# The last down projection of a two-layer decoder trunk: seven of eight output tiles in two passes over the tokens, with split weights kept between the passes

## The chip, the cores and the metric

The kernel runs on one core of one Trainium2 chip. The metric is the device time of one execution in microseconds (us). A core has a matrix engine (TensorE, "PE" in the profile), a vector engine (VectorE, "DVE"), a scalar engine (ScalarE, "ACT"), a general engine (GpSimd, "POOL") and a queue processor that issues transfers (SyncE, "SP"). Matrix products accumulate in eight PSUM banks of 128 partitions x 512 float32; everything else lies in SBUF.

## The reference

Two layers of a decoder trunk over 512 tokens with 1024 channels. What matters here is the end of each layer, the SwiGLU block with 2816 hidden units, and the norm behind the last layer:

```python
        x = x + mix @ w_out[l]
        h = rms_norm(x, norm_ffn_w[l])
        x = x + (jax.nn.silu(h @ ffn_w_gate[l]) * (h @ ffn_w_up[l])) @ ffn_w_down[l]
    return rms_norm(x, final_norm_w)
```

`rms_norm` divides each token by the root of the mean square of its 1024 channels, so no token of the output is known before all channels of that token are.

## The kernel before

**Layout.** Activations stand with channels on the partitions: `x[0..7]` are eight tiles of 128 channels x 512 tokens. The 22 tiles of hidden units (`KF`) have the tokens along their free side too. Each float32 product is made of three products of rounded halves (`mm3`, L447 to L452: high weights by high activations, high by low, low by high). A weight tile therefore comes by a DMA into a `wraw` buffer (`w_load`, L337 on, five buffers, SP's queue), ACT casts its high half `whi` (L256), and POOL or DVE subtracts for the low half `wlo` (L257). PE then takes 128 columns of `whi` or `wlo` as its loaded weights and streams 256 or 512 tokens past them.

**The feed-forward block** of each layer runs the list `steps`: hidden tiles 0 to 3 by plain products (`hidden_plain`), then the down projection of hidden tiles 0 and 1 (`head`) for all eight outputs, then hidden tiles 4 to 21 and the down projection of hidden tiles 2 to 17 by a scheme that replaces eight block products by seven (`step`, L1585 on: products e, t1, t2, g, h, t3, t4 in PSUM pool `pm`; t4 of one step is put off until `finish()` in the next), and last the down projection of hidden tiles 18 to 21 (`rest`): `down_plain(1)`, L1650 on. Its products accumulate in pool `pd`, which has four PSUM banks. For each output tile it takes the next split weights (`w_next`), makes 4 x 3 matmuls per token range, adds the sum to `x[m]` (L1665), squares the result on ACT (`ssq_add`, L220), adds the squares up in `ssq` on DVE (L222) and scales `x[m]` by the norm's weight on ACT (L1675). Output tile 0 takes its weights in two runs of two hidden tiles; between them `finish()` makes the last t4, and with it hidden tile 21.

**The order of the last layer** comes from `down_order` (L260): output tiles 0 to 5 over all tokens, then tiles 6 and 7 over the first 256 tokens, then tiles 6 and 7 over the last 256 tokens. For the second half the weights of tiles 6 and 7 are loaded and split a second time.

**The end of the kernel.** For one half of the tokens, `rstd_sum` (L226 on) sums the squares over channels by matmuls with one column (L230), scales the sum on DVE (`ms`, L234) and takes the power -1/2 on POOL (`rst`, L212). `leave` (L1637 on) spreads the result over the partitions by matmuls (`rstd_spread`, L241), copies it to SBUF on ACT (`rsb`, L245), multiplies the eight tiles, five on DVE (L1647) and three on POOL (L1645), and issues eight output DMAs, alternately from SP and ACT (L1648). The first half's sum is written behind the matmuls of tile 6's second half, its `leave` behind those of tile 7's second half; the second half's come after all.

**Weights ahead of time.** `items` is the list of all split weights in order, `pieces` that of all DMAs. `w_next` hands out item i, splits the next two, and within a feed-forward block splits up to `AHEAD` = 5 items ahead, but only items of the seven-product scheme (tuples of two). Those are spread over two SBUF pools of four slots, `wsp` and the block's own `ffw` (the list `extra`); plain items use `wsp` alone. An item of the scheme that is a difference of weight blocks (`s1`, `s2`, `s4`) is computed by DVE into a `pd` bank.

**Who sets the order.** The code writes instructions in the order described, and the program is built with a planner that orders each engine's instructions by its own estimates of their durations (`schedule_with_timeline_sim=True`). The order on an engine can thus differ from the order in the text of the kernel.

Of the kernel before, what the change touches and what calls it, by code (L numbers as in the profile page):

```python
# [8 lines left out]
F32R = mybir.dt.float32r  # L9
# [7 lines left out]
P = 128  # L17
T = 512
NB = T // P
D = 1024  # L20
KD = D // P
# [5 lines left out]
DEPTH = 2  # L27
# [3 lines left out]
EU, ET = 0, 0  # L31
N_OUT = 4
R_SUM = [1, 0]
TAIL = 2
CONF_POOL = 7
CHUNK_K = 2
ARENA = 43
# [10 lines left out]
AHEAD = 5  # L48
# [89 lines left out]
def kernel(  # L138
# [15 lines left out]
    V, S, GP, PE = nc.vector, nc.scalar, nc.gpsimd, nc.tensor  # L154
# [5 lines left out]
    wsp = ctx.enter_context(tc.tile_pool(name="wsp", bufs=4))  # L160
# [89 lines left out]
        S.activation(xh[k], x[k], AF.Copy, scale=col(wcol + k))  # L250
        V.scalar_tensor_tensor(xl[k], x[k], col(wcol + k), xh[k].bitcast(F32), op0=MUL, op1=SUB)  # L251

    def split_w(r, n=512, eng=GP):
        hi = wsp.tile([P, 528], F32R, name="whi")
        lo = wsp.tile([P, 528], F32R, name="wlo")
        S.copy(hi[:, :n], r)  # L256
        eng.tensor_tensor(lo[:, :n], r, hi[:, :n].bitcast(F32), op=SUB)  # L257
        return hi, lo

    def down_order(l):  # L260

        full, hv = slice(0, T), [slice(0, T // 2), slice(T // 2, T)]
        n = TAIL if l == DEPTH - 1 else 0
        return [(m, full) for m in range(KD - n)] + [(m, c) for c in hv for m in range(KD - n, KD)] * (n > 0)

    pieces, items = [], []
# [16 lines left out]
    def plain_order(l, end):  # L285
        return down_order(l) if end else [(m, slice(0, T)) for m in range(KD)]
# [5 lines left out]
    for l in range(DEPTH):  # L292
        for nm in ORDER:
            if nm == "gg":
                for g in range(2):
                    plain(wg[l, g], 4 * (G + 2 * H))
            elif nm in T_GROUPS:
                for g in range(2):
                    plain(wt[l, 2 * T_GROUPS.index(nm) + g], 4 * G)
            else:  # L300
                plain(wc[l, C_TILES.index(nm)], KD * P)
        for m, g in OUT_ORDER:
            plain(wo[l, m][:, g * 4 * P:(g + 1) * 4 * P], 4 * P)
        left = None
        for what, *n in steps:
            if what == "plain":
                for n_m, (m, _) in enumerate(plain_order(l, *n)):
                    for r in runs(*n, n_m == 0):
                        plain(wd[l, m][:, r[0] * P:(r[-1] + 1) * P], len(r) * P)
                        if left is not None:  # L310
                            items.append(("d", left))
                            left = None
                continue
            if what == "hidden":
                two = [wf[l, 2 * n[0] + q] for q in range(2)]
                if n[0] < N_PLAIN:
                    for ap in two:
                        plain(ap, KD * P, (V, GP))
                    continue
            else:  # L320
                part, q = n
                k0 = HEAD + part * PART
                two = [wd[l, m][:, k0 * P:(k0 + PART) * P] for m in (2 * q, 2 * q + 1)]
            pj = len(pieces)
            pieces.extend((ap, KD * P) for ap in two)
            for u in ("a", "s1", "d", "s2", "b", "s4", "s3"):
                if u != "d":
                    items.append((u, pj))
                elif left is not None:
                    items.append((u, left))  # L330
            left = pj
    raws, halves, sums = {}, {}, {}
    pos = [0, 0, 0]
# [14 lines left out]
    def slots(pool):  # L348
        return held.setdefault(id(pool), [])
# [37 lines left out]
    def w_split(upto):  # L387
        while pos[1] < min(upto, len(items)):
            i, it = pos[1], items[pos[1]]
            if len(it) == 3:  # L390
                p, n, eng = it
                h = n // 2 if n > 1024 else 512
                if len(slots(wsp)) + (n + h - 1) // h > 4:
                    return
                w_load(p + 1)
                r = raws.pop(p)
                late = i >= len(items) - 2 * TAIL
                halves[i] = []
                for a in range(0, n, h):
                    slots(wsp).append(i)  # L400
                    halves[i].append(split_w(r[:, a:min(a + h, n)], min(h, n - a), V if late and a == 0 else eng[a > 0]))
            else:
                pools = [q for q in (*extra, wsp) if len(slots(q)) < 4]
                if not pools:
                    return
                w_load(it[1] + 2)
                s_item(i, *it, min(pools, key=lambda q: len(slots(q))))
            pos[1] += 1

    def w_next():  # L410
        i = pos[2]
        pos[2] += 1
        for q in held.values():
            q[:] = [n for n in q if n >= i]
        p = piece_of(items[i])
        w_split(i + 1)
        assert i in halves
        w_load(p + 3)
        w_split(i + 2)
        while pos[1] < min(i + 1 + AHEAD, len(items)) and len(items[pos[1]]) == 2 and extra:  # L420
            n = pos[1]
            w_split(n + 1)
            if pos[1] == n:
                break
            w_load(piece_of(items[n]) + 3)
        return halves.pop(i)
# [1014 lines left out]
    for l in range(DEPTH):  # L1441
# [47 lines left out]
        with tc.tile_pool(name=f"ffp{l}", bufs=1, reuse_waits="tile") as ffp, \  # L1489
# [160 lines left out]
            def down_plain(rows):  # L1650
                order = plain_order(l, rows)
                js = (head, rest)[rows]
                for n_m, (m, c) in enumerate(order):
                    ps = pd.tile([P, T], F32, name="pd")[:, c]
                    for r in runs(rows, n_m == 0):
                        hv = w_next()
                        for n, k in enumerate(r):
                            ph, pl = hid[k]
                            mm3(ps, *hv[n // 4], n % 4, ph[:, c], pl[:, c], k == js[0], k == js[-1])
                        finish()  # L1660
                    if rows and l + 1 == DEPTH and n_m == KD:
                        rstd_sum(range(NB // 2), ssq)
                    if rows and l + 1 == DEPTH and n_m == KD + 1:
                        leave(0)
                    V.tensor_tensor(x[m][:, c], x[m][:, c], ps, op=ADD)  # L1665
                    if not rows:
                        continue
                    if l + 1 < DEPTH:
                        split_x(m, o + NV + V_NMIX)
                        ssq_add(m)  # L1670
                        nc.sync.dma_start(xs[m * P:(m + 1) * P, :], x[m])
                    else:
                        end = n_m == len(order) - 1
                        sq = ssq_add(m, end, c)
                        S.activation(x[m][:, c], x[m][:, c], AF.Copy, scale=col(V_FIN + m))  # L1675
                return sq if rows and l + 1 == DEPTH else None
# [99 lines left out]
```

## Time and profile before

| | |
|---|---|
| time, median of 3 runs | 1346.11 us (1344.49 to 1348.75) |
| the profiled execution: its time | 1343.3 us |
| its span, first to last instruction | 1341.5 us |
| mean granted PE clock | 0.978 of full speed |
| PE busy | 1288.5 us, 96% |
| DVE, ACT, POOL busy | 67%, 52%, 60% |
| DMA | 124.53 MB, mean 93 GB/s |

The profile reads one execution on the chip. Busy times of PE add up overlapping instructions, since matmuls are pipelined: from one matmul's start to the next one's is the better measure of its price. In a timeline a row has its start, its duration, engine, line, operation, output and inputs, shapes and count, and in brackets how long the engine stood idle before it and what ended that idle time. A view of windows gives each engine's busy time in a stretch, with the granted PE clock ("PEclk") and the share of the DMA engines.

### The profile page before, as it was taken

Reading aid. Unit: us, or ns where it says so; the run is one execution under the profiler, and the core shown is the slowest. Engines: PE = TensorE matmul, PEld = TensorE weight load, DVE = VectorE, ACT = ScalarE, POOL = GpSimd, SP = SyncE. Lnnn points to the kernel's source line nnn. Section 1 sums busy time; section 2 is a strip of 40 time slices with the busy share of each in tenths; the row PEclk is TensorE's granted clock in tenths of the full one; section 3 lists DMA queues with packets and bytes.
Section 4 is the critical chain, followed back from the end, with each engine's and each line's share of the span. In section 5 each row is a group of like instructions: output and inputs, shape, how many; then the busy total and the mean of one; then the engine's idle time right before and its main releaser. Section 6 shows DMA issues by size and latency. Waiting matters only on the chain.

```text
span 1341.5 us, 23755 instructions
## 1 busy us (share of the span) xinstructions
PE 1288.5 (96%) x8984; PEld 1176.6 (88%) x8984; DVE 895.0 (67%) x1569; ACT 703.9 (52%) x1454; POOL 802.4 (60%) x669
## 2 busy tenths in 40 slices
PE   8899988999999999999999998989999999999996
PEld 6788987978889999999878887888788999999995
DVE  5652769646888857776466357676559787678645
ACT  5453454535556655665446344535445566566554
POOL 5376674844366765676445766748634667566662
PEclk8899988999999999999999998989999999999998
DMA  7224210134143332332433222102422333233332
GB/s 261 68 70 115 66 40 9 33 109 134 38 151 96 110 98 92 108 113 80 154 130 95 74 78 70 29 1 64 146 86 88 101 124 112 85 125 96 106 87 71
DMA packets 60243, 124.53 MB, mean 93 GB/s; under 512 B 17504, under 2 KB 26976, under 8 KB 60128
## 3 DMA queue, kind: packets, MB, share of 16 engines
q1 hardware_dynamic: 58688, 121.83, 29.6%
q8 instruction: 71, 1.16, 0.4%
q10 hardware_dynamic: 1440, 1.18, 0.3%
q14 instruction: 44, 0.36, 0.1%
HBM read 116.17 MB, written 6.82 MB: 92 GB/s over the span
## 4 chain that ended last, share of the span: by engine, by line
PE 82%; DVE 9%; POOL 3%; ACT 3%; issue 2%; DMA 1%; POOLq 0%; SPq 0%; ACTq 0%; DVEq 0%
PE pm L450 12%; PE pm L452 12%; PE pm L451 12%; PE pd L450 10%; PE pd L451 10%; PE pd L452 10%; PE pd L480 3%; PE pd L479 3%; PE pd L478 3%; PE pm L1147 1%; POOL wlo L257 1%; DVE x L1250 1%; PE pm L886 1%; DVE ph L1518 1%; PE pm L1040 1%
## 5 line engine op out<-in xcount | busy, mean ns | idle before, releaser
L257 POOL TENSOR_TENSOR wlo<-wraw,whi 128x512 fp32r<-128x512 f32 (+2 forms) x192 | 255.0, 1335 | 248.3 <-ACT whi L256 246.8
L380 POOL TENSOR_TENSOR wlo<-wraw,whi 128x512 fp32r<-128x512 f32 x208 | 276.3, 1346 | 103.1 <-ACT whi L379 93.2
L450 PE MATMUL pm<-bh,whi 128*128 128x256 f32 x1008 | 283.1, 283 | 6.6 <-ACT pm L1599 3.1
L451 PE MATMUL pm<-bl,whi 128*128 128x256 f32 x1008 | 280.8, 280 | 0.0
L452 PE MATMUL pm<-bh,wlo 128*128 128x256 f32 x1008 | 276.8, 280 | 0.0
L256 ACT CAST whi<-wraw 128x512 fp32r<-128x512 f32 (+2 forms) x212 | 125.2, 598 | 195.7 <-PE pd L451 124.3
L450 PEld LDWEIGHTS pm<-bh,whi 128*128 128x128 f32 x1008 | 189.7, 188 | 11.4 <-ACT pm L1599 4.8
L451 PEld LDWEIGHTS pm<-bl,whi 128*128 128x128 f32 x1008 | 190.1, 189 | 0.5
L452 PEld LDWEIGHTS pm<-bh,wlo 128*128 128x128 f32 x1008 | 187.9, 189 | 0.4 <-DVE wlo L380 0.3
L450 PE MATMUL pd<-xh,whi 128*128 128x512 f32 x416 | 166.5, 402 | 4.2 <-DVE pm L935 2.3
L451 PE MATMUL pd<-xl,whi 128*128 128x512 f32 x416 | 166.3, 401 | 1.3 <-DVE xl L251 1.3
L452 PE MATMUL pd<-xh,wlo 128*128 128x512 f32 x416 | 165.7, 400 | 0.0
L379 ACT CAST whi<-wraw 128x512 fp32r<-128x512 f32 x208 | 126.4, 626 | 48.8 <-PE pm L451 41.9
L380 DVE TENSOR_TENSOR wlo<-pd,whi 128x512 fp32r<-128x512 f32 x156 | 107.0, 687 | 43.3 <-ACT whi L379 41.1
L379 ACT CAST whi<-pd 128x512 fp32r<-128x512 f32 x156 | 92.1, 590 | 78.4 <-PE pm L451 30.0
L374 POOL TENSOR_TENSOR wraw<-wraw 128x512 f32<-128x512 f32 x52 | 69.6, 1339 | 70.7 <-DVE pd L362 52.3
L478 PE MATMUL pd<-whi,xh 128*128 128x256 f32 (+1 forms) x320 | 94.5, 297 | 7.3 <-DVE ar L583 6.2
L450 PEld LDWEIGHTS pd<-xh,whi 128*128 128x128 f32 x416 | 79.5, 191 | 23.2 <-ACT ar L1050 2.4
L451 PEld LDWEIGHTS pd<-xl,whi 128*128 128x128 f32 x416 | 79.5, 191 | 20.1 <-DVE xl L251 2.9
L452 PEld LDWEIGHTS pd<-xh,wlo 128*128 128x128 f32 x416 | 79.6, 191 | 17.6
L479 PE MATMUL pd<-wlo,xh 128*128 128x256 f32 (+1 forms) x320 | 94.5, 296 | 0.0
L480 PE MATMUL pd<-whi,xl 128*128 128x256 f32 (+1 forms) x320 | 93.7, 295 | 0.0
(354 smaller groups left out, 3113.5 us busy)
## 6 DMA issues: line engine op xcount, KB each, us to landing
wraw<-in_wf_dram SPq DMA_DIRECT2D x88, 512.0 KB, 3.7
wraw<-in_wc_dram SPq DMA_DIRECT2D x35, 512.0 KB, 3.6
wraw<-in_wd_dram SPq DMA_DIRECT2D x32, 512.0 KB, 3.6
wraw<-in_wt_dram SPq DMA_DIRECT2D x16, 512.0 KB, 3.5
wraw<-in_wo_dram SPq DMA_DIRECT2D x32, 256.0 KB, 2.6
x<-in_xt_dram SPq DMA_DIRECT2D x16, 256.0 KB, 4.5
wraw<-in_wd_dram SPq DMA_DIRECT2D x16, 256.0 KB, 2.7
wraw<-in_wd_dram SPq DMA_DIRECT2D x20, 128.0 KB, 2.0
```

The costliest lines, as they stand in the source:

```text
L256: S.copy(hi[:, :n], r)
L257: eng.tensor_tensor(lo[:, :n], r, hi[:, :n].bitcast(F32), op=SUB)
L374: GP.tensor_tensor(src, c, a, op=SUB)
L379: S.copy(hi, src)
L380: eng.tensor_tensor(lo, src, hi.bitcast(F32), op=SUB)
L450: PE.matmul(ps, hi[:, w], ah, start=first, stop=False, skip_group_check=shared)
L451: PE.matmul(ps, hi[:, w], al, start=False, stop=False, skip_group_check=shared)
L452: PE.matmul(ps, lo[:, w], ah, start=False, stop=last, skip_group_check=shared)
L478: PE.matmul(o, xh[k][:, tk], hi[:, w], start=(k == 0 and b % per == 0), stop=False)
L479: PE.matmul(o, xh[k][:, tk], lo[:, w], start=False, stop=False)
L480: PE.matmul(o, xl[k][:, tk], hi[:, w], start=False, stop=(k == KD - 1 and b % per == per - 1))
L886: PE.matmul(pq[:, ct * 2 * P:(ct + 1) * 2 * P], kq[ct][rr_, b, 0, :], kq[ct][rr_, b, :, :], start=True, stop=True)
```

## The change

`TAIL` goes. In the last layer the order of the last down projection becomes: output tile 0 over all tokens, tiles 1 to 7 over the first 256 tokens, then tiles 1 to 7 over the last 256. The split weights of tiles 1 to 7 are kept in their slots from the first pass to the second (`kept`, and `w_next(keep)`, which doesn't give the slots of the last `keep` items free), so those of tiles 6 and 7 are no longer loaded and split twice: 9 pieces in place of 11. Plain items of at most 512 columns may now lie in `ffw` too, whichever of the two pools has more room, and are split up to five items ahead in a feed-forward block, as those of the scheme are. This holds in both layers, for the down projections of `head` and of `rest`. Every second one of the last eight items has its low half made by DVE. The first half's sum is written behind the matmuls of the first tile of the second pass (`n_m == KD`), its `leave` behind those of the fourth (`n_m == KD + 3`).

```diff
-TAIL = 2
...
-    def split_w(r, n=512, eng=GP):
-        hi = wsp.tile([P, 528], F32R, name="whi")
-        lo = wsp.tile([P, 528], F32R, name="wlo")
+    def split_w(r, n, pool, eng):
+        hi = pool.tile([P, 528], F32R, name="whi")
+        lo = pool.tile([P, 528], F32R, name="wlo")
...
         full, hv = slice(0, T), [slice(0, T // 2), slice(T // 2, T)]
-        n = TAIL if l == DEPTH - 1 else 0
-        return [(m, full) for m in range(KD - n)] + [(m, c) for c in hv for m in range(KD - n, KD)] * (n > 0)
+        if l < DEPTH - 1:
+            return [(m, full) for m in range(KD)]
+        return [(0, full)] + [(m, c) for c in hv for m in range(1, KD)]
...
-                for n_m, (m, _) in enumerate(plain_order(l, *n)):
+                for n_m, (m, c) in enumerate(plain_order(l, *n)):
+                    if c.start:
+                        continue
...
                 h = n // 2 if n > 1024 else 512
-                if len(slots(wsp)) + (n + h - 1) // h > 4:
+                pool = wsp
+                if n <= 512 and extra:
+                    pool = min((*extra, wsp), key=lambda q: len(slots(q)))
+                if len(slots(pool)) + (n + h - 1) // h > 4:
                     return
...
-                late = i >= len(items) - 2 * TAIL
+                late = i >= len(items) - KD and i % 2
...
-    def w_next():
+    def w_next(keep=0):
+
         i = pos[2]
         pos[2] += 1
         for q in held.values():
-            q[:] = [n for n in q if n >= i]
+            q[:] = [n for n in q if n >= i - keep]
...
-        while pos[1] < min(i + 1 + AHEAD, len(items)) and len(items[pos[1]]) == 2 and extra:
+        while pos[1] < min(i + 1 + AHEAD, len(items)) and extra and (len(items[pos[1]]) == 2 or items[pos[1]][1] <= 512):
...
                 js = (head, rest)[rows]
+                kept = {}
                 for n_m, (m, c) in enumerate(order):
                     ps = pd.tile([P, T], F32, name="pd")[:, c]
                     for r in runs(rows, n_m == 0):
-                        hv = w_next()
+                        if c.start:
+                            hv = kept[m]
+                        else:
+
+                            hv = kept[m] = w_next(len(kept) if c.stop < T else 0)
+                            if n_m == 0:
+                                kept.clear()
                         for n, k in enumerate(r):
                             ph, pl = hid[k]
                             mm3(ps, *hv[n // 4], n % 4, ph[:, c], pl[:, c], k == js[0], k == js[-1])
                         finish()
                     if rows and l + 1 == DEPTH and n_m == KD:
                         rstd_sum(range(NB // 2), ssq)
-                    if rows and l + 1 == DEPTH and n_m == KD + 1:
+                    if rows and l + 1 == DEPTH and n_m == KD + 3:
                         leave(0)
```

More of the change, by code (lines that the diff above doesn't have):

```diff
@@ L396, in w_split @@
                 r = raws.pop(p)
-                late = i >= len(items) - 2 * TAIL
+                late = i >= len(items) - KD and i % 2
                 halves[i] = []
                 for a in range(0, n, h):
-                    slots(wsp).append(i)
-                    halves[i].append(split_w(r[:, a:min(a + h, n)], min(h, n - a), V if late and a == 0 else eng[a > 0]))
+                    slots(pool).append(i)
+                    halves[i].append(split_w(r[:, a:min(a + h, n)], min(h, n - a), pool, V if late and a == 0 else eng[a > 0]))
             else:
```

## The prediction

> **What bounds the kernel now.** I read the page first, then the windows around the end, then each engine's timeline there. The page, busy shares and chain that ended last:
>
> ```profile
> PE 1288.5 (96%) x8984; PEld 1176.6 (88%) x8984; DVE 895.0 (67%) x1569; ACT 703.9 (52%) x1454; POOL 802.4 (60%) x669
> ...
> PE 82%; DVE 9%; POOL 3%; ACT 3%; issue 2%; DMA 1%; POOLq 0%; SPq 0%; ACTq 0%; DVEq 0%
> ```
>
> PE has the chain for 82% of the span. A change that neither takes matmuls away nor fills PE's pauses can gain only where PE stands still. The view of windows shows where that is at the end:
>
> ```profile
> 1308.00:1314.00 6.00, 5.05 (x29) 4.05 (x27) 0.82 (x2) 0.58 (x1) 0.00 (x0) 1.00 0.00 0
> 1314.00:1320.00 6.00, 6.00 (x27) 4.91 (x28) 4.98 (x8) 4.60 (x9) 2.56 (x2) 1.00 0.18 45
> 1320.00:1328.00 8.00, 8.00 (x60) 7.57 (x59) 7.18 (x14) 7.72 (x16) 0.00 (x0) 1.00 0.00 0
> 1328.00:1335.00 7.00, 3.15 (x22) 2.73 (x20) 2.64 (x9) 1.48 (x4) 3.44 (x5) 0.82 0.41 134
> 1335.00:1341.50 6.50, 0.04 (x1) 0.00 (x0) 1.75 (x5) 0.37 (x1) 2.09 (x3) 0.50 0.55 182
> ```
>
> The columns are stretch, length, PE, PEld, DVE, ACT, POOL, clock, DMA. PE is full until 1328 but for 0.95 us around 1313. From 1328 to the end, 13.5 us, no engine is full: that is a chain of small steps. PE's timeline gives its pieces:
>
> ```profile
> 1305.39 0.40 PE L451 MATMUL pd<-ph,whi 128*128 128x512 f32 x1
> ...
> 1310.72 0.39 PE L450 MATMUL pd<-ph,whi 128*128 128x512 f32 x1
> 1310.95 0.28 PE L450 MATMUL pm<-bh,whi 128*128 128x256 f32 x1
> ...
> 1312.22 0.28 PE L452 MATMUL pm<-bh,wlo 128*128 128x256 f32 x1
> 1312.33 0.39 PE L451 MATMUL pd<-ph,whi 128*128 128x512 f32 x1
> 1312.56 0.40 PE L452 MATMUL pd<-ph,wlo 128*128 128x512 f32 x1
> 1313.90 1.19 PE L450 MATMUL pd<-ph,whi 128*128 128x512 f32 x4 [0.95 <-ACT ph L1517]
> ...
> 1316.79 0.39 PE L450 MATMUL pd<-ph,whi 128*128 128x512 f32 x1
> ...
> 1319.76 0.39 PE L452 MATMUL pd<-ph,wlo 128*128 128x512 f32 x1
> ...
> 1325.11 0.28 PE L450 MATMUL pd<-ph,whi 128*128 128x256 f32 x1
> ...
> 1327.85 0.28 PE L452 MATMUL pd<-ph,wlo 128*128 128x256 f32 x1
> 1327.97 0.51 PE L230 MATMUL pm<-cs,ssq 128*128 128x1 f32 x4
> 1329.83 0.71 PE L241 MATMUL pm<-cs,rst 128*128 128x128 f32 x4 [1.35 <-POOL rst L212]
> 1330.37 0.50 PE L230 MATMUL pm<-cs,ssq 128*128 128x1 f32 x4
> 1330.74 0.58 PE L230 MATMUL pm<-cs,sq 128*128 128x1 f32 x4
> 1333.82 1.22 PE L241 MATMUL pm<-cs,rst 128*128 128x128 f32 x4 [2.50 <-POOL rst L212]
> ```
>
> The last large matmul starts at 1327.85. Behind it both halves' statistics run one behind the other: sum (L230) and spread (L241) of the first half, then of the second. The other engines, first DVE, then ACT, then POOL:
>
> ```profile
> 1328.17 0.42 DVE L1665 TENSOR_TENSOR x<-x,pd 128x256 f32<-128x256 f32 x1 [0.64 <-PE pd L452]
> ...
> 1328.84 0.15 DVE L234 TENSOR_SCALAR ms<-pm 128x2 f32<-128x2 f32 x1
> 1330.98 1.75 DVE L1647 TENSOR_TENSOR x<-x,pm 128x256 f32<-128x256 f32 x5 [1.98 <-ACT rsb L245]
> 1332.64 0.15 DVE L234 TENSOR_SCALAR ms<-pm 128x2 f32<-128x2 f32 x1
> 1335.48 1.75 DVE L1647 TENSOR_TENSOR x<-x,pm 128x256 f32<-128x256 f32 x5 [2.69 <-ACT rsb L245]
> ```
>
> ```profile
> 1328.62 0.42 ACT L220 ACTIVATE sq<-x 128x256 f32<-128x256 f32 x1 [0.44 <-DVE x L1665]
> ...
> 1330.57 0.37 ACT L245 COPY rsb<-pm 128x256 f32<-128x256 f32 x1 [0.99 <-PE pm L241]
> ```
>
> ```profile
> 1329.08 0.70 POOL L212 TENSOR_TENSOR rst<-ms,mhalf 128x2 f32<-128x2 f32 x1 [10.42 <-DVE ms L234]
> 1331.02 2.09 POOL L1645 TENSOR_TENSOR x<-x,rsb 128x256 f32<-128x256 f32 x3 [1.25 <-ACT rsb L245]
> 1333.07 0.69 POOL L212 TENSOR_TENSOR rst<-ms,mhalf 128x2 f32<-128x2 f32 x1
> ```
>
> The second half's squares are ready at 1328.62 + 0.42 = 1329.04, but its `ms` waits until 1332.64 behind the first half's five multiplications on DVE, and its `rst` until 1333.07 behind POOL's three. The second half stands in line behind the first on three engines.
>
> **The change part by part.** The profiled execution took 1343.3 us for a span of 1341.5, so 1.8 lie around it; the median is 1346.1, 2.8 more. I make the sum against the profiled one and carry the difference over to the median.
>
> *The end (gain).* The first half is complete after the first pass, 7 tiles before the last matmul, and its `leave` is written four tiles before the end. Its multiplications, copy and DMA issues then lie beside matmuls. The last half's chain stands alone. From the start of the last large matmul: add to `x` at 0.32 (1328.17), square from 0.77 to 1.19 (1328.62), sum of the squares 0.58 with a pick-up of about 0.04, to 1.81; `ms` 0.04 + 0.15, to 2.00; `rst` 0.09 + 0.70, to 2.79; spread 0.05 + 0.71, to 3.55; copy 0.03 + 0.37, to 3.95; first multiplication at 3.99. Before, it is 1335.48 - 1327.85 = 7.63. What follows (multiplications, DMAs, 1341.5 - 1335.48 = 6.02) is the same. **-3.64.**
>
> For the spread I took the first row (0.71 at 1329.83), not the second (1.22 at 1333.82). PE had stood for 1.35 us before the one and 2.50 before the other, and the clock was 0.82 and then 0.50 in the two last windows. In the new chain PE stands for under a microsecond between square and sum and about one before the spread, like the first row. The Trainium skill, "TensorE: Matmul & The Clock Gate", Part 1 on the clock gate, puts the step at a window of about 3.4 us with little activity, free-running, after which PE has half its clock. The trace agrees with a halving (0.50). By that rule a window that falls badly could still halve the spread: my sum would then be 0.5 smaller.
>
> *PE's stream (loss).* Tiles 1 to 5 change from 12 matmuls of 512 tokens to 24 of 256. Between 1316.79 and 1319.76 lie 13 steps of 512, 0.228 each; between 1325.11 and 1327.85 lie 23 of 256, 0.119 each. A pair costs 0.010 more, 5 x 12 = 60 pairs **+0.6**. Sum and spread of the first half, which stood behind the last matmul, now stand in the stream: 1330.74 - 1330.37 = 0.37 and 1330.37 - 1329.83 = 0.54, **+0.9**; the chain that feeds them (about 2.8 us from add to `rst`) is covered by three tiles of 12 x 0.119 = 1.43.
>
> *The pause at 1313 (open).* Hidden tile 21 comes from the t4 product, the 12 matmuls from 1310.95 to 1312.22:
>
> ```profile
> 1305.99 0.43 DVE L1609 TENSOR_TENSOR pm<-pm,u 128x256 f32<-128x256 f32 x1 [2.00 <-ACT u L1608]
> 1312.53 0.70 DVE L1622 TENSOR_TENSOR pm<-pm,sg 128x512 f32<-128x512 f32 x1 [6.11 <-PE pm L452]
> ```
>
> Until its halves are ready at 1313.90, PE fills in the products of hidden tiles 18 to 20, as far as four `pd` banks go: four tiles x 9 = 36 matmuls, 24 of them in one row from 1305.39 to 1310.72 and two behind t4; the other ten lie before that. After the change three of the four banks hold half tiles: 9 x 0.228 + 27 x 0.119 = 5.3 us of filling in place of 8.2, **2.95 less**. The matmuls aren't lost, they come later; the question is only whether PE stands meanwhile. After ten early ones some 3.1 are left. To be covered are the wait before t4 (the filling starts at 1305.39, L1609 ends at 1306.42, 1.0) and that from t4's last matmul to 1313.90, 1.7. So 3.1 would cover 2.7 if the planner split it well: -0.95 (the pause goes). If, as now, nearly all of it is put ahead of t4, the pause becomes about 1.5: +0.5. Below both, if t4 itself could not start before 1310.9, the whole 2.95 would show. I take **+0.5**, the order of the row, and keep -0.95 and +2.95 as ends. Behind it PE needs a fifth bank about 1.8 us after 1313.90 in place of 2.9, while the add that frees the first is no earlier than before:
>
> ```profile
> 1315.59 2.48 DVE L1665 TENSOR_TENSOR x<-x,pd 128x512 f32<-128x512 f32 x4 [1.02 <-PE pd L452]
> ```
>
> One add is 0.62; I give that **+0.2**, between 0 and 0.6.
>
> *Weights.* The first pass takes a weight tile every 1.43 us instead of every 2.8. With eight slots and five items ahead, they can be split in the stretch from 1305 to 1313, where DVE, ACT and POOL are nearly idle (0.82, 0.58 and 0.00 busy of 6 us from 1308). Two pieces fewer are split. ACT and DVE were off the path there, so this is worth 0; if the cover fails, a cast and a subtraction (below 2 us) show once.
>
> *Elsewhere.* The earlier splitting also holds for the `head` down projection in both layers and for `rest` in the first. PE, as the windows show, stands for almost nothing there, while DVE is full:
>
> ```profile
> 1010.00:1020.00 10.00, 10.00 (x44) 8.10 (x44) 10.00 (x19) 5.25 (x11) 3.00 (x2) 1.00 0.08 26
> 1020.00:1030.00 10.00, 10.00 (x45) 8.15 (x44) 10.00 (x20) 5.01 (x12) 3.38 (x5) 1.00 0.18 52
> 1030.00:1040.00 10.00, 9.85 (x49) 8.01 (x48) 9.83 (x20) 5.83 (x14) 7.73 (x8) 1.00 0.70 213
> ```
>
> There is nothing to gain and something to lose: the scheme's differences s1 and s2 are now made about four items earlier, on a full DVE, and hold `pd` banks that the `head` tiles want. I take 0; the ends are -1 and +6 (two layers, two tiles of 6 x 0.228 = 1.4 each, that PE would wait for).
>
> **Sum:** -3.64 + 0.6 + 0.9 + 0.5 + 0.2 = **-1.4 us**, 1341.9 against 1343.3, or **1344.7** against the median of 1346.1.
>
> **The rivals.**
>
> *1. The pause goes.* The planner puts t4 ahead of the filling, and banks don't hold PE up: -1.4 - 0.95 - 0.5 - 0.2 = -3.1, 1343.0. For it: 3.1 us of filling for 2.7 of waits. Against: the order of before, 24 in a row ahead of t4, though L1609 was done at 1306.42.
>
> *2. Half tiles starve PE (the other side).* At 1305 to 1314 the four `pd` banks are filled with half as much work, and t4's start is set by something other than the row of matmuls ahead of it. The 2.95 show in full instead of 0.5: -1.4 + 2.45 = +1.0, 1347.2, slower than before. It decides from a pause 1.9 longer than now. For it: PE did have all 36 fillers in and still stood for 0.95. Against: nothing that t4 reads is seen to end later than 1306.42.
>
> *3. The `head` stage pays.* Banks taken by s1 and s2 hold PE up near 1035 and at the same place of the first layer, and the shifted order reaches into the second layer's mixers. +4 or so on the sum, 1349. Against it, PE could take the scheme's products meanwhile, which don't need `pd`.
>
> *4. It doesn't do what it says:* the planner leaves the first half's `leave` behind the last matmul. Then 7.63 stays and PE's stream costs 0.6 + 0.5 + 0.2: +1.3, 1347.4. Against: those squares are complete some 8 us before the end.
>
> **How the numbers follow.** Forecast 0.55, rival 1 0.20, rival 2 0.14, rival 3 0.08, rival 4 0.03. A measurement of this kernel tells about 0.3%, 4.0 us, from no change (its three runs lie 4.3 apart). Even rival 1 is only 0.23%, so faster by over 0.3% needs rival 1 and luck in the medians or a shift elsewhere: 0.15. Slower by over 0.3% is most of rival 3 and a little of 2 and 4 with the runs' spread: 0.12. Within: 0.73. The range takes rival 1 with a microsecond elsewhere and the medians' scatter at the low end (1340.5), rivals 2 and 3 at the high end (1349).
>
> **What would show it.** Right: L1647 and L1645 for the first half before the last L452; from the last L452 to the second L1647 about 4.0; matmuls of 256 at 0.119 with L230 and L241 among them; fewer `pd` matmuls ahead of t4. The pause before hidden tile 21's products separates forecast (about 1.5), rival 1 (near 0) and rival 2 (near 3.9). PE's busy time from 1000 to 1060 and in the first layer's same stage judges rival 3. The prediction would be wrong by a last chain much over 4 (an engine late with work from the second pass: ACT has there seven squares of 0.42, seven scalings and four DMA issues), or by any shift over 4 us ahead of 1290, which I cost at nothing.

## The result, and the profile after

| | before | after |
|---|---|---|
| time, median of 14 runs each | 1344.87 us (1343.39 to 1348.75) | 1351.91 us (1348.09 to 1358.29) |
| ratio | 1 | 1.0055, 95% interval 1.0043 to 1.0067 |
| profiled execution, its span | 1343.3, 1341.5 us | 1356.9, 1355.1 us |

The change makes the kernel slower by 0.55%, 7.0 us between the medians. The forecast was 1.4 us faster, and its range ended at 1349.0. The profiled execution of after is one of its long ones, 5 us above its median. So the difference of the two profiles, 13.6 us, is more than the change costs; I use the profiles for where and how, and the medians for how much.

The page of after: busy times, and the chain that ended last.

```profile
PE 1299.9 (96%) x9044; PEld 1189.4 (88%) x9044; DVE 899.2 (66%) x1579; ACT 706.6 (52%) x1462; POOL 788.3 (58%) x667
...
PE 84%; DVE 9%; ACT 3%; POOL 2%; issue 1%; DMA 0%; POOLq 0%; ACTq 0%; SPq 0%; DVEq 0%
```

The page alone hides it: PE's share is 96% as before. The waits of PE, the view for the first layer's feed-forward block and then for the second layer's (engine, line, what it waited for: us in total, times, longest):

```profile
PE pd L456 <- DVE x L1678: 4.7, 1, 4.7
```

```profile
PE pd L456 <- DVE x L1678: 5.1, 1, 5.1
...
PE pd L456 <- ACT ph L1523: 1.4, 1, 1.4
PE pm L229 <- DVE ssq L221: 1.3, 1, 1.3
PE pm L240 <- POOL rst L211: 1.0, 1, 1.0
```

There are two new pauses of 4.7 and 5.1 us, one in each layer: a matmul into `pd` waits for an add to `x` that has to free a bank. The windows of both places, before and then after (stretch, length, PE, PEld, DVE, ACT, POOL, clock, DMA, GB/s):

```profile
380.00:390.00 10.00, 9.87 (x62) 8.69 (x61) 10.00 (x20) 5.49 (x12) 7.18 (x7) 1.00 0.53 173
...
1040.00:1050.00 10.00, 10.00 (x77) 9.51 (x76) 8.70 (x16) 6.54 (x15) 7.17 (x7) 1.00 0.37 110
```

```profile
380.00:390.00 10.00, 5.44 (x23) 4.67 (x24) 9.33 (x16) 3.23 (x7) 4.09 (x4) 0.83 0.16 52
...
1040.00:1050.00 10.00, 4.95 (x18) 3.88 (x17) 10.00 (x17) 2.81 (x7) 4.96 (x4) 0.66 0.15 52
```

This is the `head` down projection. PE loses half of each window, the granted clock falls, and DVE stays full. The timelines of after there, PE, then DVE, then POOL:

```profile
379.49 0.39 PE L458 MATMUL pd<-ph,wlo 128*128 128x512 f32 x1
384.56 0.76 PE L456 MATMUL pd<-ph,whi 128*128 128x512 f32 x1 [4.68 <-DVE x L1678]
385.12 0.63 PE L457 MATMUL pd<-ph,whi 128*128 128x512 f32 x1
385.55 0.63 PE L458 MATMUL pd<-ph,wlo 128*128 128x512 f32 x1
...
387.26 0.41 PE L456 MATMUL pm<-bh,whi 128*128 128x256 f32 x1
```

```profile
378.17 0.68 DVE L1678 TENSOR_TENSOR x<-x,pd 128x512 f32<-128x512 f32 x1
...
380.04 1.75 DVE L364 TENSOR_TENSOR pd<-wraw 128x512 f32<-128x512 f32 x1
381.71 0.42 DVE L1540 TENSOR_TENSOR pm<-sq,pm 128x256 f32<-128x256 f32 x1
382.04 1.45 DVE L1532 TENSOR_TENSOR pm<-gs 128x256 f32<-128x256 f32 x1
383.40 0.42 DVE L1538 TENSOR_TENSOR pm<-gs,sg 128x256 f32<-128x256 f32 x1
383.74 1.27 DVE L1678 TENSOR_TENSOR x<-x,pd 128x512 f32<-128x512 f32 x2
```

```profile
379.53 1.71 POOL L382 TENSOR_TENSOR wlo<-wraw,whi 128x512 fp32r<-128x512 f32 x1
381.93 1.27 POOL L376 TENSOR_TENSOR wraw<-wraw 128x512 f32<-128x512 f32 x1 [0.69 <-POOL wlo L382]
```

And DVE of before in the same stage:

```profile
375.65 0.68 DVE L1665 TENSOR_TENSOR x<-x,pd 128x512 f32<-128x512 f32 x1
...
377.85 0.64 DVE L1526 TENSOR_TENSOR pm<-gs 128x256 f32<-128x256 f32 x1
...
378.74 1.28 DVE L1665 TENSOR_TENSOR x<-x,pd 128x512 f32<-128x512 f32 x2
...
381.20 0.67 DVE L1665 TENSOR_TENSOR x<-x,pd 128x512 f32<-128x512 f32 x1
381.79 0.89 DVE L362 TENSOR_TENSOR pd<-wraw 128x512 f32<-128x512 f32 x1
```

Before, the second and third adds come at 378.74, and `s1`, the first difference of the scheme (L362), stands behind the fourth. After, `s1` (L364) stands between the first and the second add and takes a `pd` bank; the second and third come at 383.74, five microseconds later. Not all five are `s1`. The first add is itself 2.5 later (378.17 for 375.65), though PE starts its first `head` tile only 0.66 later (374.16 for 373.50). From the first add to the second it is 5.57 in place of 3.09, 2.5 more: `s1` takes 1.67 of that (380.04 to 381.71) and the subtraction L1532, at 1.45 for the 0.64 of L1526 before, the other 0.81. PE has done four `head` tiles (24 matmuls) by 379.49, and the fifth has no bank. Behind it in PE's order stands the scheme's first product, whose weights POOL finished at 381.24 (L382). When PE goes on it has half its clock: steps of 512 tokens at 0.43 (385.12 to 385.55) where they take 0.23.

The tail of after, PE, DVE and ACT:

```profile
1325.16 0.85 PE L456 MATMUL pd<-ph,whi 128*128 128x512 f32 x4 [1.41 <-ACT ph L1523]
...
1343.81 0.28 PE L458 MATMUL pd<-ph,wlo 128*128 128x256 f32 x1
1345.44 0.58 PE L229 MATMUL pm<-cs,ssq 128*128 128x1 f32 x4 [1.35 <-DVE ssq L221]
...
1347.49 1.22 PE L240 MATMUL pm<-cs,rst 128*128 128x128 f32 x4 [1.03 <-POOL rst L211]
```

```profile
1342.07 1.74 DVE L1653 TENSOR_TENSOR x<-x,pm 128x256 f32<-128x256 f32 x5
1343.72 0.83 DVE L1678 TENSOR_TENSOR x<-x,pd 128x256 f32<-128x256 f32 x2
1344.87 0.42 DVE L221 TENSOR_TENSOR ssq<-ssq,sq 128x256 f32<-128x256 f32 x1 [0.32 <-ACT sq L219]
1346.50 0.16 DVE L233 TENSOR_SCALAR ms<-pm 128x2 f32<-128x2 f32 x1 [1.21 <-PE pm L229]
1349.15 1.75 DVE L1653 TENSOR_TENSOR x<-x,pm 128x256 f32<-128x256 f32 x5 [2.49 <-ACT rsb L244]
```

```profile
1342.52 1.86 ACTq L1654 DMA_DIRECT2D out_dram<-x  x4
1344.42 0.72 ACT L219 ACTIVATE sq<-x 128x256 f32<-128x256 f32 x2 [2.02 <-POOL x L1651]
```

The first half's statistics and multiplications do run ahead of the last matmul. From the last large matmul to the second half's first multiplication it is 1349.15 - 1343.81 = 5.34, 7.63 before and 3.99 forecast. The pause ahead of hidden tile 21 is 1.41; the forecast was about 1.5.

### The profile page after: what moved, and what is told of

It is laid out like the page before. It is cut to its first block, busy times and chain, and to the rows that moved or that the text cites. A ratio compares the mean times of both kernels' runs of the same rounds, so it can differ in the third digit from the quotient of the medians.

```text
span 1355.1 us, 23848 instructions
## 1 busy us (share of the span) xinstructions
PE 1299.9 (96%) x9044; PEld 1189.4 (88%) x9044; DVE 899.2 (66%) x1579; ACT 706.6 (52%) x1462; POOL 788.3 (58%) x667
## 4 chain that ended last, share of the span: by engine, by line
PE 84%; DVE 9%; ACT 3%; POOL 2%; issue 1%; DMA 0%; POOLq 0%; ACTq 0%; SPq 0%; DVEq 0%
PE pm L456 12%; PE pm L458 12%; PE pm L457 12%; PE pd L456 10%; PE pd L457 10%; PE pd L458 10%; PE pd L486 3%; PE pd L485 3%; PE pd L484 3%; PE pm L1153 2%; PE pm L892 1%; DVE ph L1524 1%; DVE x L1256 1%; DVE bl L1524 1%; POOL wlo L256 1%
## 5 line engine op out<-in xcount | busy, mean ns | idle before, releaser
L256 POOL TENSOR_TENSOR wlo<-wraw,whi 128x512 fp32r<-128x512 f32 (+2 forms) x190 | 243.1, 1287 | 239.4 <-ACT whi L255 231.5
L382 POOL TENSOR_TENSOR wlo<-wraw,whi 128x512 fp32r<-128x512 f32 x208 | 274.9, 1337 | 124.6 <-ACT whi L381 121.1
L382 DVE TENSOR_TENSOR wlo<-pd,whi 128x512 fp32r<-128x512 f32 x156 | 107.2, 687 | 47.7 <-ACT whi L381 46.1
L376 POOL TENSOR_TENSOR wraw<-wraw 128x512 f32<-128x512 f32 x52 | 68.8, 1323 | 72.5 <-DVE pd L364 61.9
```

The costliest lines, as they stand in the source:

```text
L376: GP.tensor_tensor(src, c, a, op=SUB)
L382: eng.tensor_tensor(lo, src, hi.bitcast(F32), op=SUB)
```

## The experiments

Theory A: the price is the earlier splitting, outside the last stage, where it puts `s1` in front of the adds on a full DVE. The rivals: the last stage itself (its banks, its weights, its tail), and, as theory B, POOL's subtraction of the head's weights, which lengthens DVE's work. The runs are told by what they ask, not in their order. All ratios are to the kernel before, run on the same chip; line numbers differ by a few between kernels (L1665, L1668, L1678 and L1681 are one line, the add to `x`).

**The last stage alone, and the rest alone.** The first kernel is the changed one, with earlier splitting and the second pool only for the last stage's items; the second is the kernel before with just these two for all other plain items.

```diff
-                if n <= 512 and extra:
+                if n <= 512 and extra and i >= len(items) - 10:
...
-        while pos[1] < min(i + 1 + AHEAD, len(items)) and extra and (len(items[pos[1]]) == 2 or items[pos[1]][1] <= 512):
+        while pos[1] < min(i + 1 + AHEAD, len(items)) and extra and (len(items[pos[1]]) == 2 or items[pos[1]][1] <= 512 and pos[1] >= len(items) - 10):
```

And to the kernel before, which also gets the changed `split_w` with its pool:

```diff
+                pool = wsp
+                if n <= 512 and extra and i < len(items) - 12:
+                    pool = min((*extra, wsp), key=lambda q: len(slots(q)))
...
-        while pos[1] < min(i + 1 + AHEAD, len(items)) and len(items[pos[1]]) == 2 and extra:
+        while pos[1] < min(i + 1 + AHEAD, len(items)) and extra and (len(items[pos[1]]) == 2 or items[pos[1]][1] <= 512 and pos[1] < len(items) - 12):
```

> The changed kernel, but the earlier splitting and the second pool hold for the ten items of the last down projection alone; everywhere else plain items are split as before. Theory A (the earlier splitting around the head down projection lets PE stand twice for 4.7 and 5.1 us): those two pauses are gone, and the time is that of the two passes alone, 1343 to 1345 us where the kernel before has 1344.9. Theory C (the two passes at the end cost the time): still 1350 to 1352.

> The kernel before, with its order of the last down projection (TAIL = 2), but with the earlier splitting and the second pool for all plain items ahead of the last down projection: the complement of e1. Theory A: the two pauses of PE behind an add to x are there, 7 to 9 us over the kernel before (1352 to 1354). Theory C: within 2 us of the kernel before.

Measured: 1343.27 us, ratio 0.9990 (0.9975 to 1.0005), and 1353.46 us, ratio 1.0063 (1.0039 to 1.0086). In the first kernel no matmul waits for an add in a `head` stage; in the second two do, 5.0 and 4.6 us. The two effects add up to the whole change (0.9990 x 1.0063 = 1.0053, measured 1.0055). So the loss lies in the earlier splitting ahead of the last stage. What the two passes are worth is less clear: -1.3 us fits the forecast, but the interval, -3.4 to +0.7 us, holds zero too. The first kernel's profile has a pause of 1.7 us in the first layer's `head` stage, behind a difference that DVE makes and not behind an add.

**Which part of the earlier splitting: the head.** The changed kernel, with the `head` projections' weights left as before; those of `rest` are still early, in both layers.

```diff
+                        if not n[0]:
+                            of_head.add(len(items))
                         plain(wd[l, m][:, r[0] * P:(r[-1] + 1) * P], len(r) * P)
...
-                if n <= 512 and extra:
+                if n <= 512 and extra and i not in of_head:
...
-        while pos[1] < min(i + 1 + AHEAD, len(items)) and extra and (len(items[pos[1]]) == 2 or items[pos[1]][1] <= 512):
+        while pos[1] < min(i + 1 + AHEAD, len(items)) and extra and (len(items[pos[1]]) == 2 or items[pos[1]][1] <= 512 and pos[1] not in of_head):
```

> The changed kernel, but the weights of the two head projections are split in wsp and no earlier than before; those of rest are still split up to five items ahead, in both layers. Theory A (the cost arises in the two head stages, where s1 and its split get ahead of the adds to x on a full DVE): no pause behind an add in either head stage, PE full at 380 to 390 and 1040 to 1050, the time within 2 us of e1_last_stage_only (1343 to 1346), ratio 0.998 to 1.001. Rival C (any earlier splitting upsets the order that the planner makes, as e6_plain_three_ahead suggests; the head is only where it is seen): the pauses may go, but the time stays above 1349, ratio 1.003 or more, with other waits in their place, above all behind the first layer's rest projection.

Measured: 1336.23 us, ratio 0.9942 (0.9922 to 0.9962). The pauses are gone, as theory A has it, and the time is lower than either theory said. The head stages are whole again:

```profile
380.00:390.00 10.00, 9.30 (x53) 7.50 (x52) 10.00 (x20) 5.41 (x13) 6.91 (x6) 1.00 0.56 197
1040.00:1050.00 10.00, 9.73 (x80) 9.37 (x78) 7.38 (x13) 7.27 (x16) 9.06 (x8) 1.00 0.41 117
```

After stands to this kernel as 1.0055 to 0.9942, 1.1% or some 15 us, and when and in which pool the head's weights are split is all that differs in the code. That is the price of splitting them early, with all that the planner's order then does behind them.

**The other part: the first layer's rest projection.** The kernel before, with that alone split early.

```diff
-                if n <= 512 and extra and i < len(items) - 12:
+                if n <= 512 and extra and i < len(items) - 12 and i not in of_head:
```

(The diff is to the kernel of e2_ahead_only; the line that splits ahead gets the same condition.)

> The kernel before, with one part of the change: only the weights of the first layer's rest projection may lie in both pools and are split up to five items ahead. The head projections of both layers and the whole last stage are as before. In e11_head_not_early, which has this part and the last stage, the stretch from the first layer's last hidden product to the first gate of the second layer's feed-forward block is 337.1 us long, 342.5 before and 341.9 in e1_last_stage_only. Theory R (the earlier splitting of that projection is a gain by itself and the parts add up): that stretch again 336 to 339 us, ratio 0.993 to 0.998, so that this part and e1's make up e11's. Rival O (the shorter stretch is a chance of the order that the planner finds for the mixers in that one kernel): the stretch 341 to 344 us, ratio 0.999 to 1.002.

Measured: 1339.17 us, ratio 0.9942 (0.9924 to 0.9961), and the stretch from the first layer's last hidden product to the second layer's first gate row is 337.1 us again: theory R. The windows of before and then of this kernel show where it gains, in the second layer's mixers:

```profile
690.00:700.00 10.00, 8.23 (x42) 6.66 (x42) 8.51 (x14) 6.05 (x10) 3.96 (x3) 1.00 0.21 57
820.00:840.00 20.00, 16.64 (x97) 13.88 (x96) 14.93 (x34) 11.43 (x23) 10.33 (x9) 0.91 0.21 59
```

```profile
690.00:700.00 10.00, 10.00 (x53) 8.28 (x52) 8.32 (x13) 5.94 (x10) 4.75 (x4) 1.00 0.27 93
820.00:840.00 20.00, 20.00 (x118) 17.36 (x116) 15.52 (x31) 14.41 (x27) 13.68 (x12) 1.00 0.27 67
```

PE's pauses of 1.8 us near 698 and of 3.4 us between 820 and 840 are gone; the waits of PE that its view lists for the whole stretch fall from 13.3 us to 9.7. This stretch is 341.9 to 343.5 us in before and in four kernels of this study that don't split that projection early, 334.3 to 337.1 in the three that split it early and the head not. In the six that split both early, the changed kernel among them, it is 338.4 to 346.8: the gain in the mixers is there in full only where the head is left alone. Against e2_ahead_only this kernel again isolates the head: 1.0063 to 0.9942, 1.2%, the second measure of the same price. How an earlier weight split opens the mixers' order I have not taken apart.

**What in the head stage costs.** Five more kernels. (a) The changed kernel, in which the scheme's items may not come earlier than before, though the head's plain ones may:

```diff
+    plain_before = []
+    for n, it in enumerate(items):
+        plain_before.append(n if len(it) == 3 else plain_before[-1])
...
-        while pos[1] < min(i + 1 + AHEAD, len(items)) and extra and (len(items[pos[1]]) == 2 or items[pos[1]][1] <= 512):
+        while pos[1] < min(i + 1 + AHEAD, len(items)) and extra and (items[pos[1]][1] <= 512 if len(items[pos[1]]) == 3 else i >= plain_before[pos[1]] - 1):
```

> The changed kernel, but an item of the seven-product scheme is split no earlier than before (only when the last plain item ahead of it is at most one item away); plain items keep the earlier splitting and the two pools. If theory A is right in its form (the scheme's difference s1 takes a pd bank and stands ahead of the adds on DVE): both pauses gone, within 2 us of e1. Theory B (the early casts and subtractions of the plain weights themselves disturb DVE and ACT): pauses stay, 1350 to 1352.

Measured: 1352.05 us, ratio 1.0050 (1.0031 to 1.0069), a miss. `s1` is behind the adds again (382.43), and the waits of PE around the first head stage are

```profile
PE pd L459 <- DVE x L1681: 1.7, 1, 1.7
PE pm L459 <- ACT whi L384: 0.8, 2, 0.5
```

So `s1`'s place makes some 3 of the 4.7 us of the pause, but the time doesn't follow. New are PE's waits for the scheme's high halves (L384); they are too short to be the rest of the cost. The stretches of the profile say where that is. This kernel's two feed-forward blocks, measured to the last hidden product and to the first half's first multiplication, are 2.3 and 2.9 us shorter than in after. But its stretch through the mixers is 344.0, 2.1 longer than in after and 6.9 longer than in e11, and PE's busy times at 690 to 700 and 820 to 840 are 8.22 and 16.64, as in before: the gain of the early `rest` is missing. So part of the cost went with `s1`, and the mixers gave it back.

(b) The changed kernel with the first scheme step's differences in `pm` banks:

```diff
+    def s_tile(pj):
+        return pm.tile([P, T], F32, name="pm") if pj in first_step else pd.tile([P, T], F32, name="pd")
...
-            src = pd.tile([P, T], F32, name="pd")
+            src = s_tile(pj)
```

> The changed kernel, but the differences s1, s2 and s4 of the first seven-product step behind the head down projection lie in banks of pool pm and not of pd. Bank theory: PE can take a fifth head tile (1.4 us) before it waits for an add, so the two pauses behind an add to x fall from 4.7 and 5.1 to about 3.3 or less, and the time by about 3 us (1348 to 1350), if pm has a bank to spare. If what counts is only that s1 and POOL's work stand ahead of the adds on DVE: the fifth tile is made but the next waits, pauses and time within 1 us of the changed kernel.

Measured: 1354.74 us, ratio 1.0064 (1.0043 to 1.0085). The first head stage's waits:

```profile
PE pm L461 <- DVE bl L1529: 2.7, 1, 2.7
PE pd L461 <- DVE x L1683: 1.7, 1, 1.7
```

PE takes a fifth tile before it waits for an add, then the other three, and then waits 2.7 us for a row of DVE that makes operand halves (`bl`, done at 389.82). This is the scheme's first product; the only scheme weights ready by then are its own, since 381.40, and the halves that it reads were made by 370.1. So what it waits for is more likely the `pm` bank which that row reads: with `s1` in `pm`, a bank of `pm` became the gate. Here too DVE frees the bank late. The two pauses together, 4.4 us, are almost as long as the one that they replace.

(c) Plain items no more than three ahead outside the last stage:

```diff
-        while pos[1] < min(i + 1 + AHEAD, len(items)) and extra and (len(items[pos[1]]) == 2 or items[pos[1]][1] <= 512):
+        while pos[1] < min(i + 1 + AHEAD, len(items)) and extra and (len(items[pos[1]]) == 2 or items[pos[1]][1] <= 512 and (pos[1] < i + 4 or pos[1] >= len(items) - 10)):
```

> The changed kernel, but plain items outside the last down projection are split at most three ahead in place of five (before: two). Theory A: s1 then stands one item earlier than before, in place of up to four; the pauses lie between those of e1 (none) and of the changed kernel (4.7 and 5.1), near 1 to 3 us each, time 1345 to 1349. If any earlier splitting costs the same: 1350 to 1352.

Measured: 1370.72 us, ratio 1.0178 (1.0151 to 1.0205), with pauses of 6.1 and 5.8 us in the head stages: a plain miss. At three ahead the cost is larger than at five, so it doesn't grow with the distance alone. Why this one is the worst stays open.

(d) and (e) The changed kernel, and e1's, with ACT copying in place of POOL's subtraction for the head's low halves; the subtraction is left out:

```diff
-        eng.tensor_tensor(lo[:, :n], r, hi[:, :n].bitcast(F32), op=SUB)
+        if part:
+            S.copy(lo[:, :n], r)
+        else:
+            eng.tensor_tensor(lo[:, :n], r, hi[:, :n].bitcast(F32), op=SUB)
```

> The changed kernel, but the low halves of the head weights are copied by ACT (the subtraction is left out there) in place of POOL's subtraction. Theory B (POOL's subtractions that now lie beside DVE's work for the first hidden tiles lengthen DVE's instructions, so DVE is some 2 us late at the first add to x): the first add comes about 2 us earlier relative to PE, and the pauses fall to about 2.5 us each. Theory A alone (order and bank of s1): pauses within 0.7 of 4.7 and 5.1.

> The same edit (low halves of the head weights copied by ACT, the subtraction left out) on e1, where the head weights are split as late as before: the control for e8. No pause behind an add, time within 1.5 us of e1. Theory B says that e8 comes within 4 us of this one, theory A that e8 stays 6 to 8 us behind it.

Measured: 1353.24 us, ratio 1.0050 (1.0030 to 1.0070), pauses of 3.8 and 3.8; and 1342.14 us, ratio 0.9970 (0.9957 to 0.9984), none. The 11 us between them stay, so POOL's subtraction of the head's weights makes about 1 us of each pause and no more. (ACT has a copy more to make in its place.)

**The tail.** Two kernels for the chain that came out at 5.3 in place of 4.0: e1 with `leave` written one tile earlier, and that with most of the first half's way out taken off DVE and ACT:

```diff
-                    if rows and l + 1 == DEPTH and n_m == KD + 3:
+                    if rows and l + 1 == DEPTH and n_m == KD + 2:
                         leave(0)
```

```diff
-                    if k % 3 == 1:
+                    if k % 4 if half == 0 else k % 3 == 1:
                         GP.tensor_tensor(x[k][:, c], x[k][:, c], rsb[:, c], op=MUL)
...
-                    (nc.sync if k % 2 else nc.scalar).dma_start(out[k * P:(k + 1) * P, c], x[k][:, c])
+                    (nc.sync if k % 2 or half == 0 else nc.scalar).dma_start(out[k * P:(k + 1) * P, c], x[k][:, c])
```

> e1, with the first half's leave written one tile earlier (behind the third tile of the second pass instead of the fourth). If the last chain is 1.3 us longer than forecast because ACT's queue waits in it for the first half's output transfers (5.3 from the last large matmul to the first multiplication instead of 4.0), that stretch falls to about 4.0 and the time is 1 to 1.5 us under e1. If the chain is long for another reason, same as e1 within 0.3.

> e4_leave_one_earlier with the first half's way out taken off the two engines that the last chain needs: of its eight multiplications six on POOL and two on DVE (three and five in e4), and its eight output DMAs all issued by SP, none by ACT. In e4 the first multiplication of the second half starts 5.51 us behind the start of the last large matmul, not 3.99 as forecast. Theory T (the chain is late because the last but one add to x stands behind five multiplications on DVE, and its square behind four DMA issues on ACT, so that ssq and the sum are late by about 0.85): ms moves from 2.85 to about 2.0 behind the last large matmul, the first multiplication from 5.5 to 4.2 to 4.7, the time 0.8 to 1.3 us below e4, about 1343 against 1344.9, ratio about 0.998. Rival U (PE's slow sum and spread, at half clock, set the chain and the engines ahead of it do not): less than 0.3 us gained. Rival V (POOL becomes the bound: the power of the second half stands behind the six multiplications): rst starts more than 0.3 us behind ms, and the chain is no shorter than 5.5.

Measured: 1344.06 us, ratio 0.9989 (0.9975 to 1.0004), chain 5.5: the planner left the first half's `leave` where it was, its first multiplication 1.7 us ahead of the last large matmul in both kernels. And 1345.13 us, ratio 1.0003 (0.9988 to 1.0018). The tail of the second, PE and DVE:

```profile
1331.92 0.28 PE L458 MATMUL pd<-ph,wlo 128*128 128x256 f32 x1
1332.76 0.58 PE L229 MATMUL pm<-cs,ssq 128*128 128x1 f32 x4 [0.56 <-DVE ssq L221]
...
1335.27 0.71 PE L240 MATMUL pm<-cs,rst 128*128 128x128 f32 x4 [1.22 <-POOL rst L211]
```

```profile
1334.09 0.16 DVE L233 TENSOR_SCALAR ms<-pm 128x2 f32<-128x2 f32 x1 [1.15 <-PE pm L229]
1336.42 1.74 DVE L1653 TENSOR_TENSOR x<-x,pm 128x256 f32<-128x256 f32 x5 [2.17 <-ACT rsb L244]
```

`ms` comes 2.17 behind the last matmul and the first multiplication 4.50: theory T for the chain. The time doesn't show the microsecond. Together with the head left alone:

> e11_head_not_early with the way out of e10_sp_and_pool_leave: the first half's leave is written one tile earlier, its multiplications are two on DVE and six on POOL, and all its output DMAs are issued by SP. In e10 that brought the second half's first multiplication from 5.51 to 4.50 us behind the start of the last large matmul, but the time did not follow. Theory T (the shorter chain counts by its 1.0 us where nothing else moves): chain 4.4 to 4.7, time 0.5 to 1.5 us below e11, ratio 0.993 to 0.994. Rival U (the rows ahead of the chain shift by as much, as in e10): chain as short, time equal to e11's within 0.5 us or above it.

Measured: 1337.95 us, ratio 0.9940 (0.9916 to 0.9964), chain 4.49, and no difference from e11 that these runs can tell. The fastest versions are e11, e12 and e13, all about 0.6% below the kernel before and 1.1% below the changed one.

## Why the prediction failed

**The sum of the last stage fits, but partly by luck.** It gave -1.4 us; alone that stage measures 0.9990 (0.9975 to 1.0005), -1.3 us, which can't be told from zero. The chain shrank by 2.3, not 3.64, and with 2.3 the same terms add up to about 0. The profiles agree with that: from the second layer's first gate row to the second half's first multiplication it is 335.7 us in before and 335.7 in e1. Of the 1.35 that are missing, 0.84 lie ahead of `ms` (1346.50 - 1343.81 = 2.69 for 1.85): the last but one add to `x` stood behind five multiplications of the first half, and its square behind ACT's four DMA issues. I had laid "multiplications, copy and DMA issues" beside matmuls without asking which later step queues behind them, and named ACT's issues only among the dangers; e10 took both away, and `ms` came 0.5 us earlier. By the rows of after, taking away only one would have gained at most 0.3: the late add ends at 1344.13 and ACT's issues end at 1344.38, just ahead of the square at 1344.42. The other 0.51 are the spread at 1.22, which I had taken at 0.71 with the halving named beside it; in e11 it took 0.77 behind waits of the same length, so the waits alone don't decide it. The pause at 1313 came as taken, 1.41 for 1.5.

**The step that failed is "Elsewhere": "I take 0".** The paragraph had the mechanism in it: `s1` and `s2` "made about four items earlier, on a full DVE", holding banks that the head's tiles want, two places, PE stopped there. Its own windows showed DVE at 10.00 of 10. With DVE full, what is put in front of an add delays it by its whole length (1.67 us for `s1` above), and four banks are four tiles of 1.4 us: the cover was about 5.5 us deep, and I never compared it with what would be moved in front of the adds. I gave the case 0.08 as rival 3, against it "PE could take the scheme's products meanwhile". That was the wrong half: PE took its matmuls in the planned order, and the product whose weights were ready at 381.24 stood behind the tile that waited for a bank until 384.56. (No run puts that product first, so what it would have saved isn't shown.) Rival 3 was right in its places, the mixers among them, and its kind; its +4 was too small for the head, whose early weights cost some 15 us. `s1`'s bank and place alone don't make that: e3 took `s1` back behind the adds and kept nearly all of the cost.

The difference of the two most alike profiles, after and e11, says where: of 15.9 us between the spans, 4.4 lie between DVE's first gate row of the first layer's feed-forward block and its last product of hidden tiles by `up` (663.9 - 345.0 for 658.7 - 344.2), 4.8 from there to the second layer's gate (1005.8 for 995.8), 5.5 from there to the first half's first multiplication (1342.1 for 1326.6), and 1.2 around them. The two pauses are 9.8 us, about what the two feed-forward blocks lose together. The 4.8 between them are the mixers, the windows of after and then of e11:

```profile
663.90:1005.80 341.90, 336.77 (x2079) 293.20 (x2079) 215.03 (x382) 161.52 (x319) 202.47 (x178) 0.95 0.27 82
```

```profile
658.70:995.80 337.10, 327.34 (x2073) 284.13 (x2073) 214.28 (x381) 161.26 (x316) 199.88 (x176) 0.98 0.27 81
```

There after waits less than e11 (4.8 us of listed waits of PE for 9.6) but at a lower granted clock, 0.95 for 0.98. Both profiles are long ones of their kernels, so that how the 15 us divide in the median isn't shown.

**And "there is nothing to gain" was wrong too.** The same paragraph saw full PE windows in the head stages and spoke for `rest` as well. The first layer's `rest` opens into the second layer's mixers, where PE stood for several microseconds before; splitting its weights early, and nothing else, gives 0.58%. So my zero stood for about -8 and +15, not for two small things. In whole: -1.3 for the last stage, -7.8 for the first `rest` (0.0058 x 1345), +15 to +16 for the heads, together +6 to +7; measured +7.0. The last two aren't independent: the head's price is measured with the early `rest` in place, and part of it is the gain in the mixers lost again.

**What stays open:** why early `head` weights take the mixers' gain away again, in e3 with PE's old waits and in after at a lower clock; why three items ahead is worse than five; and by which wait the early `rest` clears the mixers.

## What to carry to other kernels

When a rule about lookahead is loosened, list every stage it holds in, and judge each by the engine that is full there, not by PE's share: here one line gained 8 us through one projection and lost 15 through another. An engine that is full has no place for work "a little earlier": count what is moved in front of the instruction that frees the next buffer, and compare it with the buffers' depth in time. A microsecond saved in the last chain needs every engine's queue in it looked at, down to the DMA issues of the half that is already done.

## What the hardware showed

A subtraction on DVE with both inputs in SBUF and one on POOL hold each other up, and the later one pays. In after, above, POOL's L382 starts first (379.53), and `s1` takes 1.75; the 256-token difference L1532 takes 1.45 beside POOL's L376, and the same row takes 0.43 in e9 (at 375.87) with POOL idle. L382's own 1.71 starts behind a DVE subtraction of that kind, at 379.11. In e9 the same `s1` starts just ahead of POOL; DVE's row, then POOL's:

```profile
379.92 0.69 DVE L367 TENSOR_TENSOR pd<-wraw 128x512 f32<-128x512 f32 x1
```

```profile
379.94 1.83 POOL L385 TENSOR_TENSOR wlo<-wraw,whi 128x512 fp32r<-128x512 f32 x1 [1.58 <-ACT whi L384]
```

Now `s1` has its 0.69, and POOL takes 1.83 for what it does in 1.27 to 1.30 alone. The adds to `x`, with one input in PSUM, keep their 0.6 to 0.7 throughout. The Trainium skill, "SBUF — State Buffer", section "Who interferes with whom", says that a DVE instruction with two SBUF inputs contends with a GpSimd instruction that reads SBUF, and one with at most one such input, outside the two-port modes, does not; the trace agrees with both.

A pause of 4.7 us cost more than itself: 0.43 instead of 0.23 for each of the next 512-token steps until 387.26. Whether a pause costs that isn't settled by its length. In e1 a pause of 1.72 us, up to 383.90, is followed by steps of 0.42 to 0.43 (385.41 to 386.26); in e3 one of 1.72 us, up to 379.86, is followed by steps of 0.23 to 0.24 (380.17 to 381.11).
